# A decoder trunk on one core: the parts of its mixer recorded in another order, with the room of four shared groups of tiles taken in parts of their own

## The chip, the core and the metric

One Trainium2 chip, one of its cores. The core has five engines with a queue each: TensorE (PE) for matmuls, VectorE (DVE) and ScalarE (ACT) for elementwise work and reductions, GpSimd (POOL), which does little here, and SyncE (SP), whose queue issues every transfer of this kernel. Each engine takes its instructions in the order in which they stand, and waits with semaphores for the others. The metric is the device time of one execution of the whole kernel, in microseconds; the median of the runs counts.

## What is computed

Two layers, each a half-step feed-forward, a mixer of four parallel head groups, and another half-step feed-forward, on 512 positions of width 1024 in float32:

```python
def hybrid_layer(x, ...):
    x = x + 0.5 * swiglu(rmsnorm(x, ffn1_norm), ffn1_gate, ffn1_up, ffn1_down)
    z = rmsnorm(x, mix_norm) @ w_in
    (aq, ak, av, iq, ik, iw, bq, bk, bv, bg, br, cu, dcq, dckv, dkpe) = split(z)
    y_a = dsa_mixer(aq, ak, av, iq, ik, iw, ...)      # indexer, top 128, sparse attention
    y_b = gla_mixer(bq, bk, bv, bg, br, ...)          # gated linear attention
    y_c = conv_mixer(cu, ...)                         # causal depthwise convolution, 31 taps
    y_d = mla_mixer(dcq, dckv, dkpe, ...)             # latent attention
    x = x + concatenate([y_a, y_b, y_c, y_d]) @ w_out
    x = x + 0.5 * swiglu(rmsnorm(x, ffn2_norm), ffn2_gate, ffn2_up, ffn2_down)
    return x
```

## The kernel before

Activations stand transposed, the width on the 128 partitions in eight tiles X[0..7] of 128x512. Nearly every product is made of three float32r matmuls, high by high, high by low and low by high, so an operand is a pair of tiles (`xh`/`xl`, `hh`/`hl`, `yh`/`yl`, and `whl` for a weight's both halves). In the feed-forwards the weights are loaded raw and split by ACT and DVE. The weights of the mixers are split ahead of time, stored in DRAM (`kept`), and loaded from there by `fetch` into `whl` tiles, of which there are four (`WBUF`).

`mixers` consists of parts, small functions that are called by name in the order of the list ORDER (lines 50 to 53). The names that matter below:

- `index0`, `index1`: a projection `iq`, its high and low half (`iqh` by ACT, `iql` by DVE), then twelve small copies of rows by SP into four tiles `iqs`. `gates`: a projection over eight fetched weights into four PSUM tiles, called `g` in the profile (its bank names g30 to g33), copied to `z`; `index_keys` and `b_decays` (`la`, `bcum`) follow from it. `best1` to `best3`: index products `isc`, their weighted sum `sc`, and sixteen steps of MAX8 (`c`) and MATCH_REPLACE8 on DVE.
- `conv0`, `conv1`: projections `cg` and `ca`, then 31 taps, 17 on DVE (`cacc`) and 14 as a product on ACT (`ct`) and an addition on DVE (`cacd`).
- `d_latent` (`cq`, its sum of squares `cqs` over `lsq`), `d_latent_kv` (`ckv`), `d_queries` (`uq`, `dqn`, transposes `hT`, `dqT`), `d_keys` (`ukv`, `dkn`, `hT`, `dkT`), `d_attention0` to `3`: logits `dlg`, their maximum `mx`, exponential `dpr`, transposes `dpT` copied to `pts`, products `dpo` copied to `dy`, and transposes `yT` whose halves `yh`, `yl` are what the output projection reads.
- `b_heads` (`bq`, `bk`), `values` (another `g`, g20 to g23, into `vab`), `a_heads` (a third `g`, g10 to g13, into `aqk`, then `ass`), `b_scores` (`ba` into `at`), `b_chain`, `b_out`, `b_norm`, `c_out`, `a_attention0` to `3` (`alg`, `apr`, `apT`, `apo`).

After the parts `project` multiplies Y with the output weights (`wo`) and adds to X.

The order in ORDER is not the order in which the engines work. Every call only records instructions in a `Plan`. The plan knows each tile's readers and writers, and a pool for each tag. It then runs a list scheduler with modelled costs over the whole kernel, five rounds in which the ranks come from the times of the round before, and emits the best order found. Copies that may run on ACT or on DVE (`plan.either`) get their engine there. What ORDER decides is the order in which the tiles of a tag get a buffer: a tile can be taken only when all tiles of its tag that were recorded earlier have been taken:

```python
if queue[tag][-1][1] != name or not bufs[tag]:
    ok = False
    break
```

The largest tag is `big`, 37 buffers of 128x512 in SBUF. Four groups of big tiles are shared by several parts: the halves of Y (`y_pair`), the four zeroed score tiles `at`, six tiles cut into halves (`b_halves`), and the four tiles `z0` to `z3` with the relative bias (`rel_bias_tiles`). Before, the part that happens to come first in ORDER takes the room of such a group.

All arithmetic goes through one helper, so all rows of the profile have line L428, and the rows are told apart by tile names.

Of the kernel before, what the change touches and what calls it, by code (L numbers as in the profile page):

```python
# [25 lines left out]
NT = T // 128  # L26
# [20 lines left out]
WHERE = {name: tag for tag, names in WHERE.items() for name in names.split()}  # L47
GROUPS, EARLY = ((6, 7), (4, 5), (2, 3), (0, 1)), (0, 1)

ORDER = ("conv0 index1 gates index_keys d_tables index0 b_decays best3 best1 d_latent_kv conv1 d_latent "  # L50
         "best2 d_queries d_keys d_attention1 d_attention3 values d_attention0 b_heads d_attention2 "
         "b_scores3 b_scores4 b_states a_heads b_scores0 b_scores1 b_chain b_scores2 c_out b_out2 b_out1 "
         "b_out0 a_attention2 b_gates a_attention3 a_attention1 b_out3 a_attention0 b_norm").split()


AQ, AK, AV = 0, 256, 512
# [375 lines left out]
def hybrid_trunk(ctx, tc, x_in, cst, masks, onehot, relb, pcol, prow, gu17, w_uq, w_ukv,  # L432
# [27 lines left out]
    def tt(*args):  # L460

        V.tensor_tensor(*args)
# [252 lines left out]
    def mixers(l, norm, after):  # L715
# [206 lines left out]
        def d_keys():  # L922
# [19 lines left out]
            for i in range(NT):  # L942
# [6 lines left out]
                                r.to_broadcast([128, 4, 32]), OP.mult)  # L949
                head_t(st.kT, kn, pc[:96, P_DK:P_DK + 1], i)  # L950

        def d_attention(i):

            y_pair(6)
            W = 128 * (i + 1)
            y = tmp("yt", "dy", 256)
            for h in range(4):
                p = bank("dlg")
                PE.matmul(p[:, :W], st.qT[h][:96, i * 128:(i + 1) * 128], st.kT[h][:96, :W], start=True, stop=False)
                PE.matmul(p[:, W - 128:W], identb, causb, start=False, stop=True)  # L960
                mx, sm = small("mx", 1, 4), small("sm", 1, 4)
                V.tensor_reduce(mx, p[:, :W], axis=AX.X, op=OP.max, negate=True)
                e = tmp("lg", "dpr")
                S.activation(e[:, :W], p[:, :W], AF.Exp, bias=mx, accum_out=sm)
                attend(i, h, e, sm, lambda j, h: st.KV[j][:, h, 64:128], y, "d")
            y_out(y, 6, i)
# [70 lines left out]
        def b_decays():  # L1037
# [21 lines left out]
            st.cum = big("bcum")  # L1059
            copy(st.cum, pb)  # L1060

        def b_scores(n):


            if st.AT is None:
                st.AT = [big("at") for _ in range(NT)]
                for a in st.AT:
                    G.memset(a, 0.0)
            m = (LEVELS + (0,))[n]
            w, off = (2 * m, m - 1) if m else (8, 3)  # L1070
            bv = st.cum.rearrange("p (n w) -> p n w", w=w)
            e = tmp("dd", "bd")
            ev = e.rearrange("p (n w) -> p n w", w=w)
            tt(ev, bv, bv[:, :, off:off + 1].to_broadcast([128, T // w, w]), OP.subtract)
            if m:
                S.activation(ev[:, :, :m], ev[:, :, :m], AF.Exp, scale=-1.0)
                S.activation(ev[:, :, m:], ev[:, :, m:], AF.Exp)
            else:
                eq = tmp("t2", "eq")
                S.activation(eq, e, AF.Exp)  # L1080
                S.activation(e, e, AF.Exp, scale=-1.0)
            ek = tmp("t2", "ek")
            tt(ek, st.bk, e, OP.mult)
            if m:
                qe = tmp("qe", "qe", 1024)
                qv = qe.rearrange("p (c h n i) -> p c h n i", c=NT, h=4, i=m)
                for h in range(4):
                    tt(qv[:, :, h], st.bqh[h].rearrange("p (c n w) -> p c n w", c=NT, w=w)[:, :, :, m:],
                       e.rearrange("p (c n w) -> p c n w", c=NT, w=w)[:, :, :, m:], OP.mult)
                for c in range(NT):  # L1090
                    pa = bank("ba")
                    PE.matmul(pa[:, :256], ek[:, c * 128:(c + 1) * 128], qe[:, c * 256:(c + 1) * 256], start=True, stop=True)
                    at, mk = [z.rearrange("p (n w) -> p n w", w=w)[:, :, m:] for z in (st.AT[c], MK[n])]
                    V.copy_predicated(at, mk, pa[:, :256].rearrange("p (n i) -> p n i", i=m))
                return
            for g in range(2):
                qe = tmp("qe", "qe", 1024)
                qv = qe.rearrange("p (c h i) -> p c h i", c=2, h=4)
                t = slice(g * 256, g * 256 + 256)
                for h in range(4):  # L1100
                    tt(qv[:, :, h], st.bqh[h][:, t].rearrange("p (c i) -> p c i", c=2),
                       eq[:, t].rearrange("p (c i) -> p c i", c=2), OP.mult)
                for c in (2 * g, 2 * g + 1):
                    pa = bank("ba")
                    PE.matmul(pa, ek[:, c * 128:(c + 1) * 128], qe[:, c % 2 * 512:c % 2 * 512 + 512],
                              start=True, stop=True)
                    V.copy_predicated(st.AT[c], MK[n], pa)
# [22 lines left out]
                st.VAB.append(v)  # L1130

        def b_halves():
            if st.half is None:
                st.half = [big(name) for name in ("bth", "bth", "bst", "bst", "bon", "bon")]
                st.half = [t[:, n * 256:n * 256 + 256] for t in st.half for n in range(2)]

        def b_gates():
            b_halves()
            for c in range(NT):
                brv, th = st.z3[c][:, 56:312], st.half[c]  # L1140
                S.activation(th, brv, AF.Tanh, scale=0.5)
                V.scalar_tensor_tensor(th, th, 1.0, brv, op0=OP.add, op1=OP.mult)
                tt(th.rearrange("p (h c) -> p h c", h=4), th.rearrange("p (h c) -> p h c", h=4),
                                gB[:, None, :].to_broadcast([128, 4, 64]), OP.mult)

        def b_chain():

            b_halves()
            st.ST = ST = [None]
            for c in range(3):  # L1150
                pS = bank("bS")
                PE.matmul(pS[:, :256], st.kdt[:, c * 128:(c + 1) * 128], st.VAB[c][:, 256:512], start=True, stop=True)
                sn = st.half[4 + c]
                V.tensor_tensor(sn, pS[:, :256], bmask, OP.mult)
                if c:
                    V.scalar_tensor_tensor(sn, ST[c], st.eb[:, c * 128 + 127:c * 128 + 128], sn, op0=OP.mult, op1=OP.add)
                ST.append(sn)
            st.bss = small("bss", 16)
# [26 lines left out]
        def c_out():  # L1185
# [8 lines left out]
            for n in range(2):  # L1194
# [5 lines left out]
                copy(hi, th, 0.5)  # L1200
                V.scalar_tensor_tensor(lo, th, 0.5, hi.bitcast(F32), op0=OP.mult, op1=OP.subtract)

        def a_attention(i):

            st.Z = st.Z or rel_bias_tiles()
            y_pair(0)
            W = 128 * (i + 1)
            y = tmp("yt", "ay", 256)
            for h in range(4):
# [10 lines left out]

        parts = dict(gates=gates, index_keys=index_keys, d_latent=d_latent, d_latent_kv=d_latent_kv, d_tables=d_tables, d_queries=d_queries,
                     d_keys=d_keys, b_heads=b_heads, a_heads=a_heads, b_decays=b_decays, b_states=b_states,
                     values=values, b_gates=b_gates, b_chain=b_chain, b_norm=b_norm, c_out=c_out)
        for part, ns in ((index, range(2)), (best, range(1, NT)), (conv, range(2)), (b_scores, range(5)),
                         (b_out, range(NT)), (d_attention, range(NT)), (a_attention, range(NT))):
            for n in ns:
# [154 lines left out]
```

## Time and profile before

| | us |
|---|---|
| timed runs | 2067.83, 2080.63, 2087.24 |
| their median | 2080.63 |
| the profiled execution's own time | 2065.81 |
| its span, from first to last instruction | 2064.0 |

The mean granted clock of TensorE over the span is 0.985. The span falls into the feed-forward and the mixer of the first layer (mixer from about 382 to 681 us), two feed-forwards, the mixer of the second layer (about 1400 to 1700 us), and the last feed-forward. In rows of instructions the columns are start, length, engine, line, operation, output<-inputs, shapes and count; idle time ahead of an instruction and the one that ended it stand in brackets. In groups the columns are busy time, mean ns of one, and idle time ahead with what ended it. A matmul of 512 columns has a mean length of 391 ns in such rows, since the next one starts before it ends.

### The profile page before, as it was taken

The numbers are of one execution on the slowest core, as the hardware profiler recorded it, in microseconds if no ns is written. First come the engines' busy times: TensorE is split into PE (matmuls) and PEld (weight loads), VectorE is DVE, ScalarE is ACT, GpSimd is POOL, SyncE is SP. The second block draws the span as 40 slices with busy tenths as digits, with TensorE's granted clock in tenths as the row PEclk, the third lists the DMA queues.
The fourth block names the chain that finished last, engine by engine and source line by source line (L and its number), as shares of the span: only waits on it lengthen the run. The fifth ranks groups of instructions, "written<-read, shape, count | busy, mean of one in ns | idle before, by whom it ended". The sixth has DMA issues, their size and how long they took to land.

```text
span 2064.0 us, 25409 instructions
## 1 busy us (share of the span) xinstructions
PE 2008.4 (97%) x9078; PEld 1632.2 (79%) x9078; DVE 1316.6 (64%) x2808; ACT 802.0 (39%) x1563; POOL 7.9 (0%) x20
## 2 busy tenths in 40 slices
PE   8999999999889999999999999999989999999999
PEld 6888888787657888888888888888767688888887
DVE  7565656669997745454674546457799975454444
ACT  5343334356444433233443434333653443232222
POOL 0000000000000000000000000000000000000000
PEclk9999999999899999999999999999999999999999
DMA  8676756553133435353464747435523232323232
GB/s 299 236 273 202 249 185 208 156 178 117 66 108 116 150 102 179 117 185 108 147 215 152 227 124 248 144 118 178 168 92 103 72 103 91 104 84 109 91 105 82
DMA packets 110850, 309.10 MB, mean 150 GB/s; under 512 B 13122, under 2 KB 24676, under 8 KB 110724
## 3 DMA queue, kind: packets, MB, share of 16 engines
q1 hardware_dynamic: 110724, 307.49, 45.9%
q8 instruction: 71, 1.16, 0.2%
q14 instruction: 55, 0.45, 0.1%
HBM read 238.62 MB, written 65.67 MB: 147 GB/s over the span
## 4 chain that ended last, share of the span: by engine, by line
PE 90%; DVE 7%; ACT 2%; DMA 1%; issue 0%; SPq 0%; DVEq 0%; ACTq 0%
PE gu L428 47%; PE dn L428 23%; PE g L428 5%; PE wo L428 4%; DVE sc L428 1%; PE alg L428 1%; DMA whl<-kept 1%; PE ca L428 1%; DVE c L428 1%; PE cg L428 1%; PE apo L428 1%; PE iq L428 1%; PE dpo L428 1%; PE dlg L428 1%; DVE at L428 1%; PE uq L428 1%
## 5 line engine op out<-in xcount | busy, mean ns | idle before, releaser
L428 PE MATMUL gu<-xh,whl 128*128 128x512 f32 x2816 | 829.7, 391 | 9.8 <-ACT whl L428 7.1
L428 PEld LDWEIGHTS gu<-xh,whl 128*128 128x128 f32 x2816 | 529.9, 188 | 122.1 <-ACT whl L428 7.2
L428 ACT ACTIVATE whl<-raw 128x512 fp32r<-128x512 f32 (+1 forms) x523 | 308.5, 592 | 695.3 <-PE gu L428 383.7
L428 PE MATMUL gu<-xl,whl 128*128 128x512 f32 x1408 | 499.8, 391 | 0.0
L428 DVE TENSOR_TENSOR whl<-raw,whl 128x512 fp32r<-128x512 f32 x576 | 369.7, 646 | 160.8 <-ACT whl L428 155.7
L428 PE MATMUL dn<-hh,whl 128*128 128x512 f32 x1408 | 426.6, 389 | 0.0
L428 PEld LDWEIGHTS dn<-hh,whl 128*128 128x128 f32 x1408 | 264.1, 188 | 57.0 <-issue 1.5
L428 PEld LDWEIGHTS gu<-xl,whl 128*128 128x128 f32 x1408 | 265.2, 188 | 55.6 <-issue 0.5
L428 PE MATMUL dn<-hl,whl 128*128 128x512 f32 x704 | 258.8, 390 | 0.0
L428 DVE SCALAR_TENSOR_TENSOR x<-dn,x 128x512 f32<-128x512 f32 x128 | 87.8, 689 | 147.6 <-PE dn L428 147.3
L428 PEld LDWEIGHTS dn<-hl,whl 128*128 128x128 f32 x704 | 132.1, 188 | 28.8 <-issue 1.5
L428 DVE TENSOR_TENSOR fg<-gu,rbc 128x512 f32<-128x512 f32 x88 | 60.7, 689 | 124.3 <-PE gu L428 120.4
L428 DVE TENSOR_TENSOR fu<-gu,rbc 128x512 f32<-128x512 f32 x88 | 60.6, 688 | 97.6 <-PE gu L428 97.6
L428 PE MATMUL g<-whl,xh 128*128 128x512 f32 (+1 forms) x384 | 104.1, 388 | 10.0 <-DMA whl<-kept 8.0
L428 DVE TENSOR_TENSOR khl<-kraw,khl 128x512 fp32r<-128x512 f32 (+1 forms) x124 | 81.6, 666 | 47.2 <-ACT khl L428 46.9
L428 ACT ACTIVATE khl<-kraw 128x512 fp32r<-128x512 f32 (+1 forms) x121 | 73.5, 610 | 90.0 <-DMA kept<-khl 27.4
L428 ACT ACTIVATE hh<-fu 128x512 fp32r<-128x512 f32 x87 | 55.0, 632 | 96.1 <-DVE fu L428 95.8
L428 PEld LDWEIGHTS g<-whl,xh 128*128 128x128 f32 x384 | 70.1, 197 | 23.4 <-DMA whl<-kept 10.3
L428 PE MATMUL wo<-yh,whl 128*128 128x512 f32 x256 | 80.6, 407 | 0.0
L428 DVE TENSOR_TENSOR hl<-fu,hh 128x512 fp32r<-128x512 f32 x88 | 60.7, 690 | 27.4 <-ACT hh L428 26.7
L428 ACT ACTIVATE fg<-fg 128x512 f32<-128x512 f32 x88 | 55.2, 627 | 30.2 <-DVE fg L428 27.2
L428 DVE TENSOR_TENSOR fu<-fu,fg 128x512 f32<-128x512 f32 x88 | 60.5, 687 | 2.1 <-ACT fg L428 0.7
(324 smaller groups left out, 2005.6 us busy)
## 6 DMA issues: line engine op xcount, KB each, us to landing
raw<-gu SPq DMA_DIRECT2D x176, 512.0 KB, 4.1
kept<-khl SPq DMA_DIRECT2D x108, 512.0 KB, 4.1
whl<-kept SPq DMA_DIRECT2D x108, 512.0 KB, 3.7
raw<-dn SPq DMA_DIRECT2D x96, 384.0 KB, 3.2
kraw<-wt SPq DMA_DIRECT2D x44, 256.0 KB, 4.0
kraw<-wg SPq DMA_DIRECT2D x32, 256.0 KB, 4.0
kraw<-wo SPq DMA_DIRECT2D x32, 256.0 KB, 3.9
raw<-dn SPq DMA_DIRECT2D x32, 256.0 KB, 2.8
```

What stands on the lines that cost most here:

```text
L428: call(*args, **kw)
```

## The change

ORDER gets a new sequence, and four new names in it. Each of the four shared groups is now taken in a part of its own: `d_room` (Y of attention D), `b_zero` (the score tiles and their zeroing by POOL), `b_halves`, and `a_bias` (the bias tiles with their loads, and Y of attention A). Nothing is computed in another way.

```diff
-ORDER = ("conv0 index1 gates index_keys d_tables index0 b_decays best3 best1 d_latent_kv conv1 d_latent "
-         "best2 d_queries d_keys d_attention1 d_attention3 values d_attention0 b_heads d_attention2 "
-         "b_scores3 b_scores4 b_states a_heads b_scores0 b_scores1 b_chain b_scores2 c_out b_out2 b_out1 "
-         "b_out0 a_attention2 b_gates a_attention3 a_attention1 b_out3 a_attention0 b_norm").split()
+ORDER = ("index0 conv0 gates index1 d_tables index_keys b_decays best3 best2 best1 d_latent d_latent_kv "
+         "d_queries d_keys d_room d_attention3 b_heads conv1 values b_zero d_attention0 d_attention2 "
+         "d_attention1 b_scores3 b_scores4 b_scores0 a_heads b_states b_scores1 b_scores2 c_out b_halves "
+         "a_bias b_chain b_out3 b_out0 a_attention2 b_gates a_attention0 a_attention3 b_out2 b_out1 "
+         "a_attention1 b_norm").split()
...
+        def d_room():
+            y_pair(6)
+
         def d_attention(i):
-            y_pair(6)
             W = 128 * (i + 1)
...
+        def b_zero():
+            st.AT = [big("at") for _ in range(NT)]
+            for a in st.AT:
+                G.memset(a, 0.0)
+
         def b_scores(n):
-            if st.AT is None:
-                st.AT = [big("at") for _ in range(NT)]
-                for a in st.AT:
-                    G.memset(a, 0.0)
...
         def b_halves():
-            if st.half is None:
-                st.half = [big(name) for name in ("bth", "bth", "bst", "bst", "bon", "bon")]
-                st.half = [t[:, n * 256:n * 256 + 256] for t in st.half for n in range(2)]
+            st.half = [big(name) for name in ("bth", "bth", "bst", "bst", "bon", "bon")]
+            st.half = [t[:, n * 256:n * 256 + 256] for t in st.half for n in range(2)]
...
         def b_gates():
-            b_halves()
...
         def b_chain():
-            b_halves()
...
+        def a_bias():
+            st.Z = rel_bias_tiles()
+            y_pair(0)
+
         def a_attention(i):
-            st.Z = st.Z or rel_bias_tiles()
-            y_pair(0)
```

Three places show how the emitted order moves. The first is SP's queue in the first mixer, where the loads of the eight weights of `gates` stand (`whl<-kept`, 128x344, two loads each); `iqs<-iqh` and `iqs<-iql` are the small copies of an index projection's rows. Before:

```order
L428 DMA whl<-kept_470 128x344 x2
L428 DMA whl<-kept_485 128x344 x2
L428 DMA whl<-kept_488 128x344 x2
L428 DMA whl<-kept_491 128x344 x2
L428 DMA iqs<-iqh 32x512 x8
L428 DMA iqs<-iql 32x512 x4
L428 DMA whl<-kept_506 128x344 x2
L428 DMA whl<-kept_509 128x344 x2
```

Now:

```order
L429 DMA iqs<-iqh 32x512 x8
L429 DMA iqs<-iql 32x512 x4
L429 DMA scr<-fr 128x128
L429 DMA whl<-kept_470 128x344 x2
L429 DMA whl<-kept_485 128x344 x2
L429 DMA whl<-kept_488 128x344 x2
L429 DMA whl<-kept_491 128x344 x2
L429 DMA whl<-kept_506 128x344 x2
L429 DMA whl<-kept_509 128x344 x2
```

The twelve copies of the first index projection moved from the middle of the eight weights to ahead of them; those of the second now stand behind them.

The second is PE's queue in the first mixer around the sum of squares `cqs` of the latent queries. Before:

```order
L428 MATMUL cq<-xh_725,whl 128x512
L428 MATMUL cq<-xl_726,whl 128x512
L428 MATMUL cq<-xh_725,whl 128x512
L428 MATMUL isc<-iks,iqs 128x384 x2
L428 MATMUL cqs<-ones,lsq 128x1 x4
L428 MATMUL isc<-iks,iqs 128x384 x2
L428 MATMUL uq<-shi,cqh 128x384 x4
```

Now:

```order
L429 MATMUL cq<-xl_726,whl 128x512
L429 MATMUL cq<-xh_725,whl 128x512
L429 MATMUL isc<-iks,iqs 128x384 x4
L429 MATMUL cqs<-ones,lsq 128x1 x4
L429 MATMUL ckv<-xh_683,whl 128x512
L429 MATMUL ckv<-xl_684,whl 128x512
```

Four index products instead of two stand between the last `cq` and `cqs`, and `ckv` now follows where the queries `uq` did.

The third is PE's queue at the first logits tile of attention D in the first mixer. Before, the projection around it is `values` (g_1113 to g_1116):

```order
L428 MATMUL g_1116<-whl,xh_713 128x512
L428 MATMUL hT<-ck,dkn 96x128 x8
L428 MATMUL g_1113<-whl,xh_713 128x512
L428 MATMUL g_1114<-whl,xh_713 128x512
L428 MATMUL g_1115<-whl,xh_713 128x512
L428 MATMUL g_1116<-whl,xh_713 128x512
L428 MATMUL dlg<-dkT_1021,dqT_986 128x256
```

Now:

```order
L429 MATMUL ca<-xh_695,whl 128x512
L429 MATMUL hT<-ck,dkn 96x128 x8
L429 MATMUL cg<-xh_713,whl 128x512
L429 MATMUL ca<-xh_701,whl 128x512
L429 MATMUL cg<-xl_714,whl 128x512
L429 MATMUL ca<-xl_702,whl 128x512
L429 MATMUL dlg<-dkT_997,dqT_962 128x512
```

The second convolution's projection stands there now, the whole of `values` behind it, and `bq` and `bk` of `b_heads` well ahead of it; the first head taken is one of 512 columns (`d_attention3`) instead of 256. In both layers together 27 copies and squares change their engine from DVE to ACT and ten from ACT to DVE.

More of the change, by code (lines that the diff above doesn't have):

```diff
@@ L1222, in mixers @@
                      d_keys=d_keys, b_heads=b_heads, a_heads=a_heads, b_decays=b_decays, b_states=b_states,
-                     values=values, b_gates=b_gates, b_chain=b_chain, b_norm=b_norm, c_out=c_out)
+                     values=values, b_gates=b_gates, b_chain=b_chain, b_norm=b_norm, c_out=c_out, b_zero=b_zero, b_halves=b_halves, a_bias=a_bias, d_room=d_room)
         for part, ns in ((index, range(2)), (best, range(1, NT)), (conv, range(2)), (b_scores, range(5)),
```

## The prediction

> **What bounds the kernel now.** I read the page first, then the busy time by stretches, then the timeline of the engines at the waits. The page has TensorE (PE) at 97% of the span:
>
> ```profile
> span 2064.0 us, 25409 instructions
> PE 2008.4 (97%) x9078; PEld 1632.2 (79%) x9078; DVE 1316.6 (64%) x2808; ACT 802.0 (39%) x1563; POOL 7.9 (0%) x20
> ```
>
> The change touches only the two mixers. The busy time of the engines is therefore cut at the mixers' own events: first matmul of the mixer, first maximum that VectorE (DVE) takes of a logits tile of attention D, last low half of Y, end of the output projection. The first row is a stretch of the feed-forward, for the price of a matmul; the six rows with clock 0.50 are the stretches at half clock. Columns: stretch, its length, busy time of PE, PEld, DVE, ACT, POOL with instructions, granted clock, DMA share, GB/s.
>
> ```profile
> 100.00:150.00 50.00, 50.00 (x222) 41.38 (x222) 30.88 (x50) 20.47 (x35) 0.00 (x0) 1.00 0.74 257
> 381.97:498.15 116.18, 109.99 (x528) 93.78 (x527) 87.67 (x250) 53.96 (x105) 0.57 (x2) 0.94 0.52 166
> 498.15:660.03 161.88, 147.94 (x737) 108.66 (x736) 146.71 (x451) 76.67 (x218) 2.11 (x5) 0.95 0.26 87
> 660.03:681.34 21.31, 21.31 (x96) 17.65 (x95) 15.75 (x26) 9.00 (x15) 0.00 (x0) 1.00 0.36 122
> 1400.31:1514.39 114.08, 107.42 (x526) 90.28 (x525) 86.94 (x247) 55.34 (x110) 0.00 (x0) 0.97 0.55 170
> 1514.39:1678.63 164.24, 149.74 (x739) 110.40 (x738) 147.18 (x445) 76.22 (x216) 1.99 (x4) 0.94 0.25 79
> 411.90:418.73 6.83, 6.04 (x21) 6.04 (x22) 4.84 (x8) 2.38 (x4) 0.00 (x0) 0.50 0.76 241
> 466.51:473.34 6.83, 6.70 (x24) 6.70 (x25) 5.65 (x31) 2.00 (x6) 0.00 (x0) 0.50 0.44 155
> 521.13:538.19 17.06, 11.57 (x40) 8.54 (x40) 15.69 (x50) 6.58 (x24) 0.13 (x1) 0.50 0.00 0
> 1432.49:1435.90 3.41, 3.41 (x14) 3.41 (x13) 2.89 (x5) 1.44 (x2) 0.00 (x0) 0.50 0.87 249
> 1487.10:1490.51 3.41, 3.13 (x10) 3.13 (x11) 3.30 (x16) 1.12 (x3) 0.00 (x0) 0.50 0.58 189
> 1538.30:1555.37 17.07, 12.10 (x38) 8.89 (x39) 16.20 (x51) 6.23 (x24) 0.00 (x0) 0.50 0.01 1
> ```
>
> In the feed-forward PE is busy for all of the 50 us: 50 us / 222 = 0.225 us a matmul, and nothing in the change can shorten that. A mixer is a relay. Up to 498.15 PE leads and DVE has 28.5 us without work (116.18 - 87.67). From 498.15 to 660.03 DVE is busy for 146.71 of 161.88 us and PE waits here and there. At the end PE alone runs the output projection. So a mixer's length is PE's way to the hand-over, then DVE's work to the last Y, then the projection; an idle PE between hand-over and last Y costs nothing as long as DVE never waits for it. These rows name the events of the first mixer and the waits of PE in both (columns: start, length, instruction; in brackets the idle time before it and who ended it):
>
> ```profile
> 381.97 0.39 PE L428 MATMUL cg<-xh,whl 128*128 128x512 f32 x1
> 412.69 0.66 PE L428 MATMUL g<-whl,xh 128*128 128x344 f32 x1 [3.52 <-DMA whl<-kept]
> 437.83 0.38 PE L428 MATMUL bcum<-ck,la 128*128 128x128 f32 x1 [0.99 <-DVE la L428]
> 466.64 0.58 PE L428 MATMUL cqs<-ones,lsq 128*128 128x1 f32 x2 [1.69 <-DVE lsq L428]
> 498.15 0.42 DVE L428 TENSOR_REDUCE mx<-dlg 128x1 f32<-128x256 f32 x1
> 526.54 0.80 PE L428 MATMUL dlg<-dkT,dqT 96*128 96x128 f32 x2 [3.61 <-DVE yl L428]
> 659.54 0.49 DVE L428 TENSOR_TENSOR yl<-yT,yh 128x128 fp32r<-128x128 f32 x2 [0.34 <-ACT yh L428]
> 1431.08 0.43 PE L428 MATMUL g<-whl,xh 128*128 128x344 f32 x1 [3.52 <-DMA whl<-kept]
> 1455.03 0.38 PE L428 MATMUL bcum<-ck,la 128*128 128x128 f32 x1 [0.99 <-DVE la L428]
> 1484.34 0.83 PE L428 MATMUL cqs<-ones,lsq 128*128 128x1 f32 x6 [1.69 <-DVE lsq L428]
> ```
>
> **The change, step by step.** It computes the same tiles with the same instructions; a net 17 copies or squares go from DVE to ACT in both layers together (27 one way, 10 the other), and the place of every part moves.
>
> *PE's way to the hand-over.* Before, 164 large matmuls that attention D does not need stand ahead of its first logits tile: 68 of `values` (g) and all 96 of the two convolutions. Now it is 124: 48 of `b_heads` (bq, bk) and 76 of the convolutions. 40 fewer x 0.225 = 9.0 us; in the second mixer 163 against 125, 38 x 0.225 = 8.6 us. Against it eight more transposes hT stand ahead of it, at 2.4 us / 16 = 0.15 each, 1.2 us:
>
> ```profile
> L428 PE MATMUL hT<-ck,dqn 128*96 128x128 f32 x16 | 2.4, 272 | 0.0
> L428 DVE SCALAR_TENSOR_TENSOR cacc<-hp,pc,cacc 128x512 f32<-128x512 f32 x32 | 23.9, 746 | 0.2
> L428 DVE TENSOR_TENSOR cacd<-cacd,ct 128x512 f32<-128x512 f32 x26 | 17.8, 685 | 0.6
> L428 DVE TENSOR_SCALAR dkT<-hT,pc 96x128 f32<-96x128 f32 x8 | 2.5, 343 | 0.9 <-ACT dkT L428 0.9
> L428 DVE CAST yh<-yT 128x128 fp32r<-128x128 f32 x7 | 2.0, 289 | 4.1 <-PE yT L428 4.1
> ```
>
> Net -7.8 and -7.4 us.
>
> *The wait of the gates.* SyncE's queue (SP) issues all loads in order:
>
> ```profile
> 401.48 0.80 SPq L428 DMA_DIRECT2D whl<-kept  x2
> 402.37 5.03 SPq L428 DMA_DIRECT2D iqs<-iqh  x8
> 407.50 2.43 SPq L428 DMA_DIRECT2D iqs<-iql  x4
> 410.03 2.93 SPq L428 DMA_DIRECT2D whl<-kept  x6
> ```
>
> Twelve small copies of the index queries take 7.46 us of the queue between the fourth and the fifth weight of `gates`, and PE stops for 3.52 us; from 411.90 to 418.73 it has half clock. Now the twelve stand ahead of all eight weights, while PE still has 48 matmuls (10.8 us) of the convolution to do, and the second twelve behind all eight. The 3.52 us go, with the half clock behind them: half of 6.83 is 3.4 in the first mixer, half of 3.41 is 1.7 in the second. I charge 1 us for a first weight that comes late behind the twelve; ends: 0, if the copies start when `index0` ends, and 4.5, one more 3.52 and 1, if the queue is held up in the same way. Sum -5.9 and -4.2 us. The last four copies of `index1` now land shortly before the fifth index product; if they are late PE waits there, up to 2 us, and I charge nothing, since some forty matmuls of g, index1 and cq stand between their issue and it.
>
> *Two small waits stay.* Between la and bcum stood 20 large matmuls (ckv and cg) and PE still waited 0.99 us; now 16 of cq and three index products stand there, so I take no change, between -1 and +1. The wait for cqs stays too: the square and the addition that it needs start at the last cq as before, four index products instead of two (0.5 us) cover a little, and DVE reaches the addition later. I take no change, between -5.1 and -3.4 us (1.69 with its half clock) and +2 (a wait of the size of the gates').
>
> *DVE from hand-over to last Y.* 403 rows of DVE before, 396 after. Added are seven taps of conv1 (4 x 0.746 + 3 x 0.685), its three steps ahead of the taps (3 x 0.69) and about 1.5 us of small copies; gone are six yh (0.289), five dkT (0.343), about 2.5 us of selection steps that now come earlier and some 1.6 us of others: 8.6 - 7.5, so +1 us; in the second mixer the same count gives +1.7. The copies that ACT takes over lie in its idle time (it is busy for 76.67 of 161.88 us); where DVE has nothing else it waits for one as in the row at 659.54, 0.34 us, for six at most 2 us a mixer, charged at nothing because other DVE rows stand between most of them.
>
> *New waits of DVE behind the hand-over.* This is the price of the 40 matmuls: they now run between the first logits and the end of `a_heads`. These rows are that stretch before:
>
> ```profile
> 498.15:579.61 81.46, 72.89 (x358) 56.24 (x357) 77.86 (x213) 39.91 (x106) 2.11 (x5) 0.90 0.24 82
> 1514.39:1597.40 83.01, 73.46 (x356) 56.14 (x355) 79.05 (x215) 38.89 (x103) 1.99 (x4) 0.90 0.24 77
> ```
>
> PE is idle for 8.6 us of it and loses half of 11.57, 5.8, to the half clock: 14.4 lost, 67.1 of work. With 7.8 more that is 75. Summed over the order at this trace's durations, DVE comes to the first tile of `a_heads` after 72 us of its own work, and PE finishes that tile after 65 (the other three take the last 10 us); ACT copies and squares it in between. So PE may lose about 6 us before DVE stands still. I take 9 us lost (convolution and `values` now fill the waits between transposes), so DVE waits 3 us a mixer; ends: 0, and 8.4 if PE loses 14.4 again.
>
> *Projection.* 85 matmuls instead of 81 (88 for 84) stand behind the last Y: +0.9 us in each, between 0 and 0.9, as they only move. The zero fills, the tables of the bias and the room of the groups cost nothing of their own: POOL is busy for 7.9 us of 2064, and the four loads of the bias stand one projection weight further back in SP's queue, long ahead of attention A; if that cover went, PE would wait about as long as for the gates, 3.5 us.
>
> Sum: first mixer -7.8 - 5.9 + 1.0 + 3.0 + 0.9 = -8.8; second -7.4 - 4.2 + 1.7 + 3.0 + 0.9 = -6.0. Together -15 us against the profiled execution, whose own time is 2065.8 (span 2064.0 and 1.8 around it): 2051. The three timed runs have a median of 2080.6, 15 above it; with the profiled one the middle of four is 2074. I start between these two, at 2077: **2062 us**.
>
> [...] Half clock began at 466.51, after an idle time of 1.69 us, and lasted 6.83 us. [...]
>
> **Rivals.** *Larger gain* (2077 - 31 = 2046): DVE does not wait behind the hand-over (6 us), the wait for cqs goes with its half clock (8.5) and the gates' weights come in time (2). For it: every wait of PE there is short. Against it: the half clock at cqs came in both mixers. *Little of it arrives* (2077 - 4 = 2073): PE loses 14.4 us behind the hand-over as before, and DVE waits 8.4 in each mixer instead of 3. For it: the same dpT and yT with their waits for ACT's copies. *Slower: PE becomes the bound behind the hand-over.* The 17.06 us of half clock were harmless, because 40 matmuls fewer stood there. With two such stretches in a mixer PE loses 17 + 8.6 = 25.6, DVE waits 19.6 in each, and 39 less the 21 us gained elsewhere is +18: 2095. The point from which it decides is a loss of some 16 us a mixer. Against it: more large matmuls lie between the small ones, and the half clock began where they had run out. *Nothing changes in the front*: DVE is late itself; its two longest waits there were for ACT, not PE:
>
> ```profile
> 436.62 0.69 DVE L428 SCALAR_TENSOR_TENSOR la<-la,la 128x512 f32<-128x512 f32 x1 [4.42 <-ACT la L428]
> 441.08 0.75 DVE L428 SCALAR_TENSOR_TENSOR sc<-rl,wi,ck 128x512 f32<-128x512 f32 x1 [3.30 <-ACT rl L428]
> ```
>
> The convolution's first tap also comes about 3 us later, as index0 is ahead of it. If DVE reached the hand-over at 498 anyhow, the sum would be 0 to +4: 2079.
>
> **How the numbers follow.** A measurement of this kernel tells about 1% (21 us) from no change: three runs lie within 19. Chances: forecast 0.48, larger gain 0.20, clock rule's case 0.06, little arrives 0.12, nothing in the front 0.06, slower 0.08. The forecast's own range, 2050 to 2074, takes in DVE's wait from 0 to 8.4 and the ends of the small waits. Faster by over 1% (below 2056) are the larger gain, half of the clock case and a quarter of the forecast: 0.35; slower by over 1% (above 2098) are half of the slower rival and what I have not seen: 0.10; within 0.55. The range 2042 to 2084 leaves out the slower rival and the far side of the larger gain.
>
> **What would show it.** No idle time over 1 us ahead of g; half clock gone near the gates; from the mixer's first matmul, which stands nine feed-forward matmuls earlier, to the first logits maximum some 105 us in both mixers instead of 116 and 114; DVE idle at most 3 us more from there to the last Y. Wrong, if the hand-over is as late as before, or if DVE then waits for cg, g or ba for more than 10 us a mixer.

## The result and the profile after

The changed kernel takes 2023.47 us (median of four executions, 2020.9 to 2024.4) against 2075.70 (four executions, 2067.8 to 2087.2): a ratio of 0.974, interval 0.969 to 0.979. The forecast was 2062 with a range of 2042 to 2084; the gain is more than double what was forecast. In the experiments further down the kernel before was timed again with each set, at a median of 2067.1 to 2067.4 (19 executions each); against that the change is worth 43.6 us, and the two profiled executions (2065.81 and 2022.92) differ by 42.9. Differences from the kernel before are taken against these larger samples. Medians are over all executions; the intervals leave out executions that the clock held up.

The page of the changed kernel, its span and the shares of PE and DVE:

```profile
span 2021.1 us, 25409 instructions
PE 1986.5 (98%) x9078; PEld 1618.7 (80%) x9078; DVE 1302.4 (64%) x2791; ACT 808.2 (40%) x1580; POOL 6.9 (0%) x20
```

The busy time by stretches, cut at the same events as in the prediction (first matmul of the mixer, first maximum of a logits tile of attention D, last Y, end of the output projection; first and second mixer):

```profile
379.50:485.00 105.50, 100.14 (x502) 82.66 (x502) 82.70 (x246) 54.16 (x113) 0.77 (x3) 1.00 0.52 165
485.00:635.00 150.00, 145.68 (x766) 110.66 (x765) 144.30 (x442) 80.53 (x224) 2.05 (x5) 1.00 0.30 99
635.00:657.39 22.39, 22.39 (x100) 18.56 (x99) 16.05 (x26) 9.47 (x15) 0.00 (x0) 1.00 0.51 174
1374.29:1481.13 106.84, 102.41 (x502) 84.80 (x501) 85.14 (x251) 53.64 (x110) 0.52 (x1) 0.97 0.56 168
1481.13:1634.95 153.82, 147.74 (x767) 113.59 (x766) 144.43 (x439) 79.96 (x222) 1.93 (x4) 0.98 0.30 97
1634.95:1656.97 22.02, 22.02 (x98) 18.21 (x98) 15.15 (x24) 8.96 (x15) 0.00 (x0) 1.00 0.43 142
```

The way to the hand-over is about as long as forecast (105.50 and 106.84 us; "some 105"). The surprise is the second row of each mixer: 150.00 instead of 161.88 us, and 153.82 instead of 164.24. The forecast had made both 4 to 5 us longer. DVE's work in them is 2.4 and 2.8 us less (146.71 to 144.30, 147.18 to 144.43), and its idle time falls from 15.2 to 5.7 us and from 17.1 to 9.4.

The kernel before had one more stretch at half clock than the prediction's six rows, in its second mixer from 1623.63 to 1627.05 us; the sums below include it. In the changed kernel the first mixer has none left, the second has three short stretches, none of them at the gates and none of 17 us. The rows of these three:

```profile
1428.07:1431.48 3.41, 3.41 (x14) 3.02 (x13) 1.93 (x4) 1.61 (x5) 0.00 (x0) 0.50 0.19 78
1441.72:1445.13 3.41, 3.41 (x10) 2.75 (x10) 2.19 (x12) 2.19 (x5) 0.00 (x0) 0.50 0.03 10
1564.60:1571.43 6.83, 6.83 (x24) 5.72 (x23) 4.78 (x15) 1.06 (x4) 0.00 (x0) 0.50 0.00 1
```

The timeline of PE in the changed kernel, the rows with a wait (in brackets, with who ended it). The 3.52 us ahead of g, the 0.99 ahead of bcum and the 1.69 ahead of cqs are gone; shorter ones for ACT's rl, ahead of the index products, have come, and behind the hand-over the longest is 2.66 us. Some of these rows, the last wait of the first mixer (0.45 us) among them:

```profile
432.90 0.74 PE L429 MATMUL isc<-iks,iqs 96*128 96x512 f32 x2 [2.12 <-ACT rl L429]
438.88 0.50 PE L429 MATMUL isc<-iks,iqs 96*128 96x512 f32 x1 [1.07 <-ACT rl L429]
453.25 0.83 PE L429 MATMUL ckvs<-ones,lsq 128*128 128x1 f32 x6 [1.03 <-ACT lsq L429]
567.57 1.44 PE L429 MATMUL ba<-qe,ek 128*128 128x256 f32 x4 [1.55 <-DVE qe L429]
584.57 1.20 PE L429 MATMUL wo<-yh,whl 128*128 128x512 f32 x4 [0.45 <-ACT yh L429]
1563.99 1.51 PE L429 MATMUL ba<-qe,ek 128*128 128x256 f32 x4 [2.66 <-DVE qe L429]
```

**The stretch that the prediction did not look at.** After 584.57 (1584.89 in the second mixer) PE has no wait of over 0.25 us up to the end of the mixer. In the kernel before the last such wait ended at 610.75 (1629.60 in the second mixer), 49 us ahead of the last Y. Cut there, the stretch from hand-over to last Y reads, in the kernel before:

```profile
498.15:610.75 112.60, 98.67 (x469) 72.69 (x467) 108.14 (x308) 51.06 (x136) 2.11 (x5) 0.92 0.27 89
610.75:660.03 49.28, 49.27 (x268) 35.97 (x269) 38.57 (x145) 25.61 (x83) 0.00 (x0) 1.00 0.24 82
1514.39:1629.60 115.21, 100.71 (x471) 74.43 (x469) 110.44 (x312) 51.05 (x136) 1.99 (x4) 0.91 0.27 87
1629.60:1678.63 49.03, 49.03 (x268) 35.97 (x269) 36.74 (x134) 25.18 (x81) 0.00 (x0) 1.00 0.19 59
```

and in the changed kernel:

```profile
485.00:584.56 99.56, 95.24 (x481) 73.16 (x479) 97.70 (x266) 52.90 (x135) 2.05 (x5) 1.00 0.33 112
584.56:635.00 50.44, 50.43 (x285) 37.50 (x286) 46.59 (x177) 27.63 (x89) 0.00 (x0) 1.00 0.22 75
1481.13:1584.89 103.76, 97.71 (x481) 76.05 (x479) 98.14 (x263) 52.87 (x132) 1.93 (x4) 0.97 0.33 107
1584.89:1634.95 50.06, 50.03 (x286) 37.54 (x287) 46.29 (x177) 27.09 (x90) 0.00 (x0) 1.00 0.25 75
```

In the last 49 us ahead of the last Y of the kernel before, PE is busy for 49.27 of 49.28 us and DVE for 38.57: PE leads there already, and DVE waits. The two mixers' gain behind the hand-over, 22 us, comes from the first rows (112.60 to 99.56, 115.21 to 103.76), where PE stood idle for 14 us and had the 17 us at half clock; the last 50 us are 1 us longer than before.

The same rows have a second side. Ahead of PE's last wait DVE is nearly full in the kernel before (108.14 of 112.60 us, 110.44 of 115.21), and there the changed kernel leaves it 10.4 and 12.3 us less to do; behind that point it has 8.0 and 9.6 us more. What moved are above all steps of the index selection (`best1` to `best3`). Those on the tile `c` in the first mixer, the two stretches before and the two now:

```profile
498.15:610.75 112.60, 44.54 (x123) 0.92 0.27 89
610.75:660.03 49.28, 5.01 (x18) 1.00 0.24 82
485.00:584.56 99.56, 34.78 (x90) 1.00 0.33 112
584.56:635.00 50.44, 13.53 (x43) 1.00 0.22 75
```

In the second mixer they are 47.66 and 1.61 us before, 33.07 and 15.04 now.

### The profile page after: what moved, and what is told of

It is laid out like the page before. It is cut to its first block, busy times and chain, and to the rows that moved or that the text cites. A ratio compares the mean times of both kernels' runs of the same rounds, so it can differ in the third digit from the quotient of the medians.

```text
span 2021.1 us, 25409 instructions
## 1 busy us (share of the span) xinstructions
PE 1986.5 (98%) x9078; PEld 1618.7 (80%) x9078; DVE 1302.4 (64%) x2791; ACT 808.2 (40%) x1580; POOL 6.9 (0%) x20
## 4 chain that ended last, share of the span: by engine, by line
PE 94%; DMA 2%; DVE 2%; ACT 1%; issue 0%; SPq 0%; ACTq 0%; DVEq 0%
PE gu L429 48%; PE dn L429 24%; PE g L429 5%; PE wo L429 4%; DMA whl<-kept 2%; PE alg L429 1%; PE iq L429 1%; PE dlg L429 1%; PE apo L429 1%; PE ca L429 1%; PE cg L429 1%; PE dpo L429 1%; PE bk L429 1%; PE bq L429 1%; PE ba L429 0%; PE ckv L429 0%
```

## The experiments

Four theories. A: a mixer lasts as long as PE's work plus what PE loses, idle or at half clock, and this holds behind the hand-over too. B: the relay of the prediction, with DVE bound up to the last Y. C: the new back of the order took away DVE's waits at the end. D: the early room did it. One more, F, concerns the clock and is named with its run.

The kernels below are made of three pieces of the two orders: the front (up to `d_keys`), the middle (up to `b_scores4`), the back. Where a kernel has an old piece, the room is taken there at its first use, which is what the code before did; the old order with the four parts at those places is the old program, instruction for instruction, so the four parts by themselves move nothing. Each of these kernels is scheduled anew, so an edit also moves what it does not name: in b_dve, by the traces, some 280 of PE's 9078 instructions stand in another place than in the kernel before.

For every profile the table gives PE's idle time in both mixers (length less busy time, as in the rows above), what the half clock took (an estimate: half of PE's busy time in the stretches at 0.50, as if a matmul lasted twice as long there; the two executions of e_mid below have 90 and 195 matmuls in the same time), and the span less both. The median of the kernel before is 2067.

| kernel | median us | span us | PE idle | half clock | span less both |
|---|---|---|---|---|---|
| before | 2067.1 | 2064.0 | 41.3 | 23.1 | 1999.6 |
| changed | 2023.5 | 2021.1 | 20.2 | 6.8 | 1994.1 |
| e_front | 2052.9 | 2050.0 | 32.7 | 21.4 | 1995.9 |
| e_mid | 2059.5 | 2075.6 | 28.9 | 51.1 | 1995.7 |
| e_mid2 (the same) | 2058.8 | 2053.1 | 29.4 | 24.6 | 1999.2 |
| e_back | 2062.0 | 2058.9 | 43.4 | 22.5 | 1993.0 |
| e_fm | 2030.0 | 2027.8 | 25.0 | 3.2 | 1999.5 |
| e_rooms | 2035.1 | 2032.6 | 24.6 | 11.8 | 1996.2 |
| e_conv1 | 2053.2 | 2053.1 | 30.1 | 27.6 | 1995.4 |
| e_gates | 2078.3 | 2076.5 | 34.4 | 41.9 | 2000.1 |
| b_dve | 2062.9 | 2063.2 | 38.7 | 27.1 | 1997.5 |
| a_dve | 2042.1 | 2040.1 | 32.8 | 11.2 | 1996.1 |
| b_pe | 2077.6 | 2076.3 | 36.9 | 21.5 | 2017.8 |
| a_pe | 2042.7 | 2039.6 | 18.2 | 4.9 | 2016.5 |

The last column is PE's work in the mixers and all that lies outside them: 1993 to 2000 us in every kernel that has the same matmuls (so a difference of 5 us can't be explained from it), while the spans differ by 55 us, and some 20 us more in the two that were given 21.6 us of matmuls. That alone is bookkeeping. That it is the cause takes the runs in which one engine got more work.

### More work for one engine

b_pe: the early output projection twice.

```diff
-                        mm3(ps[d], *block(2 * d + n), *Y[k], g == groups[0] and n == 0, g == groups[-1] and n == 1)
+                        first, last = g == groups[0] and n == 0, g == groups[-1] and n == 1
+                        if groups is EARLY:
+                            mm3(ps[d], *block(2 * d + n), *Y[k], first, False)
+                            first = False
+                        mm3(ps[d], *block(2 * d + n), *Y[k], first, last)
```

> The kernel before with every product of the early output projection (groups 0 and 1 into the upper half of X) issued twice: 48 large matmuls more a mixer, which stand between 40 us behind the hand-over and the last Y; at 0.225 us they are 10.8 us of PE a mixer, 21.6 in all. The output holds these products twice. Theory A (PE's lost time; PE has no wait left in the last 50 us before the last Y): the end moves by what the added work does not find as idle time or half clock: +13 to +22 us. Theory B (the relay: DVE sets the way from hand-over to last Y, and an idle PE there costs nothing): PE has 14 us idle there, the 10.8 fit: 0 to +4.

Measured: 2077.6 against 2067.4, +10.1 (ratio 1.0038, interval 1.0024 to 1.0051). That is below A's 13 to 22 and above B's 0 to 4, so neither range holds it. By the table the profiled execution is 12.3 us longer: the last column grew by 18, PE's losses shrank by 6.

b_dve: sixteen additions a mixer twice.

```diff
-                tt(e[:, :W], st.Z[h][:, 384 - 128 * i:512], st.AM[i][:, :W], OP.add)
+                for _ in range(2):
+                    tt(e[:, :W], st.Z[h][:, 384 - 128 * i:512], st.AM[i][:, :W], OP.add)
```

> The kernel before with the sum of bias and mask of attention A issued twice (the second time over the first): 16 DVE additions of 128 to 512 columns more a mixer, by the rows of before 0.284 to 0.683 us each, 7.7 us of DVE a mixer, 15.4 in all, all of them between the scores and the last Y and on no chain of PE's. Theory A: DVE has 10 us of waits in the last 50 us before the last Y, where PE has none; the additions go there: -4 to +5 us. Theory B: DVE is bound up to the last Y, every added microsecond shows: +12 to +16.

Measured: 2062.9 against 2067.4, -4.5 (ratio 0.9972, interval 0.9956 to 0.9988). That is half a microsecond beyond A's -4 to +5; B's 12 to 16 is out. Why the kernel became a little faster was not tried. The rows from hand-over to last Y of this kernel, both mixers:

```profile
496.94:662.49 165.55, 152.06 (x738) 112.34 (x737) 150.53 (x467) 76.73 (x216) 2.11 (x5) 0.92 0.24 82
1516.97:1677.94 160.97, 148.65 (x738) 110.38 (x737) 149.81 (x460) 75.87 (x219) 2.19 (x4) 0.95 0.26 80
```

DVE is busy for 150.53 and 149.81 us instead of 146.71 and 147.18, 6.4 us more in sum. That is less than the 15.4 of the single rows, partly because rows that follow one another overlap and because the new schedule gave some other rows to ACT; the test is weaker by so much. But none of these 6.4 us showed in the time.

The same two edits in the changed kernel, a_dve and a_pe:

> The changed kernel with the same 15.4 us of DVE additions. Its PE is idle for 4 and 6 us between hand-over and last Y, its DVE for 6 and 9. Theory A with the rider that the new order leaves neither engine room there: +8 to +18. If PE alone is bound in the changed kernel: 0 to +5. Theory B: +12 to +16.

> The changed kernel with the same 96 large matmuls more (21.6 us of PE, the output holds these products twice). Theory A: with 10 us of idle PE in both stretches together and little of it where the projection stands: +16 to +22. Theory B (DVE bound up to the last Y, PE idle for 4 and 6 us there): +8 to +14.

Measured: a_dve 2042.1 and a_pe 2042.7, +18.6 and +19.3 against 2023.5. So the changed kernel has no room on either engine: with more DVE work PE's idle time goes from 20.2 to 32.8 us. B's 8 to 14 for a_pe is out; a_dve is a little over A's 18, and over B's 16.

### The three pieces of the order

e_front (the back and middle of before, and `conv1` kept in the front):

```diff
-conv0 index1 gates index_keys d_tables index0 b_decays best3 best1 d_latent_kv conv1 d_latent best2 d_queries d_keys
+index0 conv0 gates index1 d_tables index_keys b_decays best3 best2 best1 conv1 d_latent d_latent_kv d_queries d_keys
```

> The kernel before with the front of the new order alone (index0 first, gates before index1, best2 before best1, the latent of the queries before that of the keys); the second convolution stays in the front, and middle and back are those of before. Theory A (lost PE time: a mixer lasts as long as PE's work, its idle time and the half of its half clock, and from about 50 us ahead of the last Y PE has no wait left): the 3.52 us wait of the gates and its half clock go, -10 us over both mixers, between -6 and -14; the 17 us of half clock behind the hand-over stay in both. Theory B (the relay of the prediction, DVE bound up to the last Y): also -10, since the front is cut by as much. Theory C (the new back of the order is what took DVE's waits away): -10 as well, DVE idle behind the hand-over still about 15 us a mixer. This run prices the front; it does not tell A from B.

e_mid (`conv1` taken out of the old front):

```diff
-d_room d_attention1 d_attention3 values d_attention0 b_heads d_attention2 b_zero b_scores3 b_scores4
+d_room d_attention3 b_heads conv1 values b_zero d_attention0 d_attention2 d_attention1 b_scores3 b_scores4
```

> The kernel before with the middle of the new order alone: b_heads, the second convolution and values stand between the first logits of attention D, the attentions follow in the new order; front (less that convolution) and back are those of before. Theory A: the two stretches of 17 us at half clock go, and with them the 3.6 and 3.4 us waits for yl; of the 14.4 us that PE lost there 2 to 4 are left: -10 to -12 a mixer, -20 to -24 in all; the gates' 3.52 us stay. Theory B: 40 matmuls fewer in front and 3 us of DVE waits behind: -4 to -5 a mixer, -8 to -10 in all, the last Y no sooner than the hand-over moves. Theory C: as B, since the back is the old one: DVE idle behind the hand-over still about 15 us.

e_back:

```diff
-b_states a_heads b_scores0 b_scores1 b_halves b_chain b_scores2 c_out b_out2 b_out1 b_out0 a_bias a_attention2 b_gates
-a_attention3 a_attention1 b_out3 a_attention0 b_norm
+b_scores0 a_heads b_states b_scores1 b_scores2 c_out b_halves a_bias b_chain b_out3 b_out0 a_attention2 b_gates
+a_attention0 a_attention3 b_out2 b_out1 a_attention1 b_norm
```

> The kernel before with the back of the new order alone (from b_scores0 on: chain, outputs of B and attentions of A in the new order). Theory A: PE has no gap in the last 50 us of before, so what DVE waits there is worth nothing: -3 to +3 us. Theory B: no change but for small waits, -2 to +2. Theory C: DVE's waits of the last 25 us (about 8 us a mixer) go: -14 to -18 us in all.

e_fm (new front and new middle, old back):

> Front and middle of the new order, the back that of before. Theory A, if the parts add: 14 us of the front and 22 of the middle, 2067 - 36 = 2031, up to 2040 where the clock falls in the attentions of A. Theory C (the new back took DVE's waits away): 2050 or more.

Measured, against 2067.1: e_front -14.2 (ratio 0.9945, interval 0.9921 to 0.997); e_mid -7.5 in the median, with single executions from -24 to +10 (ratio 0.9893, 0.986 to 0.9926, that is -22); e_back -5.1 (0.9968, 0.9956 to 0.998); e_fm -37.1 (0.9836, 0.9795 to 0.9876). Whether the parts add up depends on the executions that are taken. By the medians they do not: 14.2 and 7.5 are 22, and e_fm has 37. Of the 17 executions of e_mid's program (five here, twelve as e_mid2 below) seven lie at 2043 to 2048, some 21 us under the kernel before, and with those 14 and 21 come near it; e_fm, too, has one of its four at 2050.6. The back brings 5 us by itself and 6.5 on top of the others; C wanted 14 to 18, A and B no more than 3, so their size was a little off, and C is out. e_front's gain is at the edge of what was expected, and does not lie where it was: its PE idles in the front for 7.3 and 6.5 us, as long as before (6.2 and 6.7; waits for rl replace that of the gates), and behind the hand-over for 9.7 and 9.2 instead of 13.9 and 14.5.

Where the middle acts is seen in the first 40 us behind the hand-over, most of attention D. First mixer of the kernel before, of e_mid, of the changed kernel, and of e_conv1, which follows:

```profile
498.15:538.15 40.00, 32.27 (x164) 24.18 (x163) 37.30 (x103) 24.14 (x68) 0.13 (x1) 0.79 0.12 40
494.24:534.24 40.00, 39.61 (x236) 31.71 (x235) 38.32 (x110) 24.22 (x71) 0.00 (x0) 1.00 0.22 70
485.00:525.00 40.00, 39.98 (x239) 32.03 (x238) 39.51 (x116) 25.83 (x75) 0.00 (x0) 1.00 0.25 80
500.46:540.46 40.00, 34.74 (x175) 24.92 (x173) 38.38 (x108) 23.11 (x69) 0.12 (x1) 0.83 0.02 3
```

With the new middle alone PE loses 0.4 us here instead of 13.5, while DVE is as busy as before. So it is in every profile: idle time and half clock together are at most 2.1 us in both mixers of the seven whose middle has the new sequence (in e_rooms without the early `b_zero`), and 7.3 us or more in the other seven.

### One part put back

e_conv1 is the changed kernel with `conv1` between `best1` and `d_latent`, the rest as changed.

> The changed kernel with one part put back: the second convolution stands in the front again, ahead of the latents, so that its 48 large matmuls (10.8 us a mixer) and its taps run ahead of the hand-over, and b_heads and values alone are left for the waits of attention D. Theory A: PE's losses behind the hand-over grow from 4 and 10 us towards the 20 and 22 of before: +8 to +15 a mixer, 2040 to 2053. If values and b_heads suffice to fill the waits: 2023 to 2030.

Measured: 2053.2, 29.8 us over the changed kernel, at the edge of A's range. Its rows of half clock in the attentions of D, first and second mixer:

```profile
514.12:527.77 13.65, 11.98 (x35) 7.42 (x35) 13.24 (x38) 5.57 (x20) 0.12 (x1) 0.50 0.00 0
1527.90:1548.40 20.50, 19.62 (x66) 14.66 (x66) 14.46 (x43) 7.15 (x21) 0.00 (x0) 0.50 0.00 1
```

The long half clock of the kernel before (17 us at 521 and at 1538) is back. b_heads and values alone do not fill PE's waits of attention D; with the 48 matmuls of the convolution among them they do. Two thirds of the gain hang on this one place. Of the 31 us that PE loses more by the table, 9 lie ahead of the hand-over and 21 behind it. The edit moves DVE's selection too: in the last 50 us ahead of the last Y its steps (`c` and `sc`) take 4.9 and 7.1 us here, 15.0 and 16.7 in the changed kernel. How much of the 29.8 us is the missing filling and how much is DVE's order was not separated by any run.

e_rooms is the changed kernel with `b_zero` and `a_bias` at the first use of their tiles (`b_halves` then stands directly ahead of `b_chain`, with nothing but `a_bias` gone from between).

> The changed kernel, with the room of the four groups taken where it was taken before: the zeroed tiles ahead of the first scores, the half tiles ahead of the chain, the tables of the bias ahead of the first attention A; nothing else moves by hand. If the order of the parts is what counts (theories A, B and C alike): within 5 us of the changed kernel, 2020 to 2030. If the early room is what counts (theory D): at least half of the gain goes, 2045 or more.

Measured: 2035.1 (2030.1 to 2038.8), 11.6 us over the changed kernel: more than A allowed, less than D. The early room is worth about a quarter of the gain in this order. PE's losses are 9.4 us larger; the wait ahead of the first wo that was 0.45 us is 2.47 now, and half clock takes 11.8 us instead of 6.8 by the table. Which of the two rooms does it, and through which tile, was not tried.

### The gates' wait by itself, and the clock

e_gates is the kernel before with two parts exchanged:

```diff
-conv0 index1 gates index_keys
+conv0 gates index1 index_keys
```

> The kernel before with two parts exchanged: gates ahead of index1, so that the second twelve copies of the index queries stand behind the eight weights of gates in SyncE's queue. The prediction's price of the gates' wait: PE's 3.52 us and the half clock behind go, -5.9 and -4.2 us, 2057. If another wait takes its place (the index products now come later to DVE and ACT): 2062 to 2070, with the wait of PE seen elsewhere in the front.

Measured: 2078.3 (2065.5 to 2082.6), 11 us slower, where both cases had it faster or equal. Up to the hand-over it does what was forecast, in the first mixer: PE waits nowhere for g, and the way is 110.33 us instead of 116.18, the 5.9 less that were forecast (the mixer begins 1.5 us later, so the hand-over comes at 493.83 instead of 498.15). In the second that way is as long as before (114.07 and 114.08 us, with a granted clock of 0.96 and 0.97). Then half clock takes 17 us, by the estimate of the table, in the attentions of A of the second mixer:

```profile
1627.30:1661.40 34.10, 34.10 (x89) 19.15 (x88) 16.15 (x56) 10.40 (x29) 0.00 (x0) 0.50 0.05 12
```

e_mid had shown two such stretches; e_mid2 is the same kernel again.

> The kernel with the new middle alone once more, unchanged, since its five times lay between 2043 and 2077 and its profile showed stretches of 24 and 34 us at half clock in the attentions of A, 29 us lost, with the waits of PE all under 1.6 us. [...] Theory F (the order of the instructions sets the clock): one group, the stretches in every profile.

Measured: twelve executions, five at 2044.6 to 2047.6, one at 2054.9, six at 2062.6 to 2065.7. That is not the one group that F says. The profile is of the execution at 2054.9; it has the first of the two stretches and lacks the second. None of the lower group was profiled. Two stretches of e_mid (2077.4), then two of e_mid2:

```profile
602.08:625.97 23.89, 23.89 (x65) 14.41 (x63) 12.47 (x42) 6.93 (x19) 0.00 (x0) 0.50 0.01 2
1626.06:1660.20 34.14, 34.14 (x90) 20.20 (x89) 16.21 (x56) 10.84 (x30) 0.00 (x0) 0.50 0.05 16
```

```profile
597.91:621.80 23.89, 23.89 (x65) 14.42 (x63) 12.44 (x42) 6.93 (x19) 0.00 (x0) 0.50 0.01 2
1626.06:1660.20 34.14, 34.14 (x195) 25.47 (x195) 29.94 (x121) 18.52 (x61) 0.00 (x0) 1.00 0.15 48
```

In the second mixer one execution runs 90 matmuls in 34.14 us, the other 195 in the same stretch at full clock. PE's idle time over both mixers is the same (28.9 and 29.4 us), the half clock took 51.1 and 24.6: the same instructions, the same idle time, and 22.5 us between the spans. It also shows once more that PE sets the end there: what it loses 30 to 60 us ahead of the last Y arrives in the time.

## Why the prediction was wrong

**The step that failed** is the bound that the prediction put on the way from hand-over to last Y: "So a mixer's length is PE's way to the hand-over, then DVE's work to the last Y, then the projection; an idle PE between hand-over and last Y costs nothing as long as DVE never waits for it." DVE is nearly full only up to 610.75 (108.14 of 112.60 us); from there to the last Y PE is, and DVE idles for 10.7 of 49.28. PE's 14 us of idle time and the 6 to 8 that the half clock took ahead of that point were therefore not free: they pushed all of PE's later work back. The prediction had the numbers (14.4 us lost in the first 81) and priced them by what DVE might wait, 3 us more a mixer. It also counted DVE's work up to the last Y as one sum, where it matters on which side of PE's last wait a step stands. Measured, what PE lost from hand-over to last Y fell from 19.7 to 4.3 us in the first mixer and from 22.2 to 9.5 in the second. Two things show that PE sets the end there: b_dve (DVE work added, no longer time) and the one program of e_mid and e_mid2 (17 us of half clock late in the second mixer arrive in the time). b_pe agrees in part, with 10 of 21.6 us.

Not shown is which change behind the hand-over brought the 22 us. The new middle fills PE's waits in attention D, in every profile that has it; but DVE was nearly full up to PE's last wait, and the new order also moves 8 to 12 us of its work a mixer, mostly selection steps, behind that point. No run holds one of the two fixed, so this share of the cause stays open.

**Term by term**, first and second mixer:

- Way to the hand-over, forecast -13.7 and -11.6: measured -12.7 and -9.2 (116.18 and 114.08, with the 2.0 us of nine feed-forward matmuls, to 105.50 and 106.84). PE's work came out at -5.5 and -7.2 (forecast -7.8 and -7.4), its idle time and half clock at -7.2 and -2.1 (forecast -5.9 and -4.2). The 40 and 38 matmuls went, and the gates' wait with them. Not foreseen were the waits for rl (2.12, 1.07 and 0.72 us in the first mixer); in the second, two stretches of 3.41 us at half clock follow on them (at 1428.07 and 1441.72), so that term came short.
- The small waits, priced at nothing: bcum and cqs went (0.99 and 1.69 us) and so did the half clock at cqs, ckvs came with 1.03. The half clock at cqs took 3.4 and 1.6 us before, so these terms were a gain, near the end that the forecast gave as -5.1 and -3.4; the waits for rl took a part of it back.
- DVE's work behind the hand-over, forecast +1.0 and +1.7: summed row by row it grew by 1.0 and 2.0 us, as counted. Its busy time, in which rows that overlap count once, fell by 2.4 and 2.8, since more of the rows overlap now.
- DVE's waits behind the hand-over, forecast +3 each: measured -9.5 and -7.7. This term alone is 23 us of the 28 between the sum of -15 and the -42.9 of the two profiled executions; it is what the failed step stands for in the sum.
- Projection, forecast +0.9 each: measured +1.1 and +0.9.
- The base: 2077 was taken; the kernel before is at 2067 in the larger samples, so the change gained 43.6 and not 53.

**The rivals.** "Larger gain" had the right side and the wrong ground: it let DVE not wait behind the hand-over, not PE lose less. "Little of it arrives" and "Nothing changes in the front" came out the other way. "Slower" had feared two stretches of 17 us at half clock behind the hand-over. The new order removes the one that there was: with `conv1`, `b_heads` and `values` between the small matmuls of attention D it is gone (e_mid), without `conv1` it is back (e_conv1). e_mid and e_gates show that such stretches do come with other orders, in the attentions of A, and that they take 12 to 17 us each by the estimate of the table. The "clock rule's case", with 0.06 in the chances, rests on what no run shows: in the kernel before half clock came at or behind the wait of 1.69 us for cqs in both mixers, and in the changed kernel it began three times with no wait of PE over 2.66 us.

**The marks**: no wait over 1 us ahead of g, and no half clock at the gates: both as said. Hand-over after some 105 us: as said (105.50 and 106.84). DVE idle at most 3 us more up to the last Y: wrong, it is 9.5 and 7.7 less. The test that would have warned is cheap: ask of every stretch not only how busy the presumed bound is on average, but from which moment the other engine has no wait left.

Left open: how the 22 us divide between PE's filled waits and DVE's moved selection steps, what the room does (e_rooms), and why the back brings 5 us.

## What to carry to other kernels

Where two engines hand work to each other, find the last wait of each ahead of the end; the engine without waits is the bound from there on, and whatever it lost earlier is in the time, even in a stretch where another engine was busier. Big independent matmuls are best kept for the stretches of small dependent ones: 48 of them moved out of attention D cost 30 us here, with all that the scheduler moved along with them. Where DVE is full ahead of that last wait, steps that nobody needs before it belong behind it; the changed kernel has them there, but no run tried that alone. A part exchanged for a good reason can lose through the clock far behind it (34.10 us at half clock in e_gates), so look at all stretches of half clock before the edit is judged.

## What the runs showed of the hardware

In the rows above with a granted clock of 0.50 the length is a multiple of 3.41 us: 3.41, 6.83, 13.65, 17.06 or 17.07, 20.50, 23.89 and 34.14 (34.10 in e_gates). The starts within one execution lie multiples of it apart, too: 411.90, 466.51 and 521.13 in the kernel before are 54.61 and 54.62 us apart, sixteen times 3.413; 1428.07, 1441.72 and 1564.60 in the changed kernel 13.65 and 122.88, four and thirty-six times. In the kernel before the matmuls of `uq` with 384 columns start 0.32 us apart in the stretch at half clock that ends at 473.34, and 0.18 us apart right behind it.

In the attentions of A half clock lasted 23.89 and 34.14 us in e_mid (65 and 90 matmuls), with PE busy for all of the time by its records. Another execution of the same program (e_mid2) ran the second of these stretches at full clock, 195 matmuls in 34.14 us. So whether it begins there differs from one execution to the next of the same program; by the estimate of the table such a stretch takes 12 or 17 us, half of its length.

In the mixers of the changed kernel half clock began three times. The nearest waits of PE ahead of it were 2.04 us (to 1426.94, half clock from 1428.07), 0.71 (to 1439.29, from 1441.72) and 2.66 (to 1563.99, from 1564.60), the last the longest of both mixers. Behind the wait of 2.12 us at 432.90, in the first mixer, there was none.
